# One 128-wide f32 product in place of two 64-wide ones, in a two-layer decoder trunk

## Chip, cores and metric

The kernel runs on one core of a Trainium2 chip. The metric is the device time of one execution in microseconds; lower is better. All arithmetic is in f32.

## What is computed

A trunk of two layers over 1024 tokens of width 1024. Layer 0 mixes by causal pooling, layer 1 by sliding-window attention; both attend to 256 memory tokens as well, and both end in a squared-ReLU MLP of width 4096. Cut to the products:

```
for l in range(2):
    if l == 1:
        kv = rmsnorm(h, kv_norm) @ w_kv                     # 1024x1024 @ 1024x512
    proj = rmsnorm(h, norm_mix[l]) @ w_in[l]                # 1024x1024 @ 1024x1024
    main, mq = proj[..., :768], proj[..., 768:]
    main_out = pool_mixer(main, ...) if l == 0 else swa_sink_attention(rmsnorm(main), k, v, sinks)
    mkv = rmsnorm(mem, mem_norm[l]) @ w_mem_kv[l]           # 256x1024 @ 1024x512
    mem_out = memory_attention(rmsnorm(mq), mk, mv)
    h = h + concat([main_out, mem_out]) @ w_out[l]          # 1024x1024 @ 1024x1024
    u = relu(rmsnorm(h, norm_mlp[l]) @ w_up[l])             # 1024x1024 @ 1024x4096
    h = h + (u * u) @ w_down[l]                             # 1024x4096 @ 4096x1024
```

## The kernel before

Activations lie transposed: 128 features on the partitions, tokens along the free dimension, in halves of 512 tokens. A product takes a weight tile of 128 inputs (partitions) by 128 outputs as the stationary operand and 512 tokens as the moving one, and adds into one bank of 128 outputs by 512 tokens. All such products go through one helper, `pair` (lines 259 to 261). It issues two matmuls, one for outputs 0 to 63, one for outputs 64 to 127, with the two halves of the weight tile and the same moving operand. Two such matmuls are called a couple here, and one matmul 64-wide by its output partitions.

Four places call it. `mm3` (line 263) runs over the input tiles k of a projection. `scores` (line 501) makes the attention scores of two heads, with 512 or 256 columns. `Stream.run` (line 893) does the MLPs and the output projection of layer 0, in seven products of blocks for eight (the order of the seven steps is `ORDER`, line 611), each unit being four couples. `plain_unit` (line 1009) does the first block of each MLP. The columns number 512, but 256 in the memory projections (`mem_layer`, 413) and in some score products.

Not all of TensorE's work goes through `pair`. Transposes are 128 wide (`transpose4`, line 273; lines 357, 445, 454, 1111). `head_stats` (line 531), `Norm.finish` (line 309) and line 435 reduce over partitions by plain f32 products 128 wide with one or two columns. The products of attention weights and values (line 587 for memory, line 1464 for the window) are written out as 64-wide matmuls, one for each head of a couple of heads.

In `Stream.run` the order of all instructions is written by hand (`tc.manual_schedule`). In the mixing stages they are placed by the framework's scheduler from the order of the code; there the short tasks of attention (`mem_attn`, `swa`, `head_stats`) are interleaved with projections by `tick`, which every couple calls with 0.43.

Of the kernel before, what the change touches and what calls it, by code (L numbers as in the profile page):

```python
# [16 lines left out]
P = 128  # L17
# [23 lines left out]
def kernel(  # L41
# [25 lines left out]
    nc = tc.nc  # L67
# [56 lines left out]
    def mm_tile():  # L124
        return mmps.tile([P, HALF], F32, tag="mm", name="mm")
# [27 lines left out]
    for wi in range(4):  # L153
        w = 2 << wi
# [102 lines left out]
    ALL = slice(0, P)  # L257

    def pair(ps, w, a, start, stop, **kw):
        for e in (slice(0, 64), slice(64, P)):  # L260
            nc.tensor.matmul(ps[e], w[:, e], a, start=start, stop=stop, **kw)  # L261

    def mm3(ps, wsel, asel, ks, us=0.43):

        n = len(ks)
        for i, k in enumerate(ks):
            w0, a0 = wsel(k, 0), asel(k, 0)
            pair(ps, w0, a0, i == 0, i == n - 1)
            tick(us)
# [231 lines left out]
    def scores(ps, st, n, khi):  # L501

        t = slice((n % 2) * P, (n % 2 + 1) * P)
        pair(ps, st[:, 0, t], khi, True, True)
# [155 lines left out]
    class Stream:  # L660
# [232 lines left out]
        def run(self, plain=()):  # L893
# [5 lines left out]
            for i in range(-len(plain), n):  # L899
# [22 lines left out]
                for k in range(4):  # L922
                    x_ = step.win[k]
                    pair(ps, w[:, 0, k, :], x_[:, 0], m in (1, 2, 7) and k == 0, k == 3, skip_group_check=True)
                    tick(0.43)
# [589 lines left out]
    for n in range(NK):  # L1515
# [6 lines left out]
        for hf in range(2):  # L1522
            ps = mm_tile()
# [10 lines left out]
    for n in range(NK):  # L1534
# [4 lines left out]
        for hf in range(2):  # L1539
            ps = mm_tile()  # L1540
# [41 lines left out]
```

## Time and profile before

| | us |
|---|---|
| median of the runs (2, from 2356.3 to 2357.81) | 2357.06 |
| the profiled execution | 2354.09 |
| its span, first to last instruction | 2352.3 |
| TensorE busy in it | 2326.8 |
| ScalarE busy | 989.6 |
| VectorE busy | 797.9 |
| GpSimd busy | 168.8 |

The span is what the profile covers. A matmul counts as busy from its start to a modelled end, and matmuls overlap, so starts tell more than busy time. PE is TensorE's matmuls, PEld its weight loads, DVE is VectorE, ACT is ScalarE, SP issues most DMAs. A row's shape "128*64 128x512" is: stationary operand of 128 partitions by 64 columns, moving operand of 128 partitions by 512 columns.

### The profile page before, as it was taken

What the parts mean: (1) busy time and instruction counts of PE and PEld (TensorE: products, weight loads), DVE (VectorE), ACT (ScalarE), POOL (GpSimd) and SP (SyncE); (2) the same over time, 40 slices, a digit from 0 to 9 for tenths busy, and PEclk for the clock granted to TensorE, in tenths of its full rate; (3) what the DMA queues carried; (4) which work ended last, traced back from release to release, by engine and by line L of the source; (5) the groups of instructions that cost most, each with busy time, mean ns of one, the idle gap of its engine ahead of it and who ended that gap; (6) DMA issues with size and microseconds to landing.
All of it is one profiled execution on the core that took longest, in us unless ns stands there. A gap on an engine that the chain in (4) does not pass through costs nothing.

```text
span 2352.3 us, 28640 instructions
## 1 busy us (share of the span) xinstructions
PE 2326.8 (99%) x11324; PEld 847.8 (36%) x11324; DVE 797.9 (34%) x1495; ACT 989.6 (42%) x2063; POOL 168.8 (7%) x226
## 2 busy tenths in 40 slices
PE   8999899999999999999999999999999999999999
PEld 4543233333333333333444443333333333333333
DVE  1363425322232152153243443433521422233141
ACT  6443454533532442454343464545423523532442
POOL 1410020000000000000322120020000000000000
PEclk9999999999999999999999999999999999999999
DMA  5302312223213213211211031214132133113201
GB/s 215 90 23 87 108 54 108 89 90 105 74 54 113 85 36 126 90 59 43 70 39 35 27 97 51 86 55 147 42 125 90 37 106 108 55 62 118 90 18 54
DMA packets 139064, 185.99 MB, mean 79 GB/s; under 512 B 20852, under 2 KB 67762, under 8 KB 138930
## 3 DMA queue, kind: packets, MB, share of 16 engines
q1 hardware_dynamic: 137458, 179.43, 23.3%
q10 hardware_dynamic: 1472, 4.73, 0.5%
q8 instruction: 90, 1.47, 0.3%
q14 instruction: 44, 0.36, 0.1%
HBM read 152.67 MB, written 31.46 MB: 78 GB/s over the span
## 4 chain that ended last, share of the span: by engine, by line
PE 97%; ACT 1%; DVE 1%; DMA 1%; issue 0%; SPq 0%; ACTq 0%
PE mm L261 54%; PE sps L261 26%; PE pv L261 12%; PE tr L273 2%; PE tr L531 1%; PE pv L1464 1%; PE pv L587 1%; PE tr L309 0%; DMA wa<-in_w_out 0%; ACT s L1431 0%; DMA g<-in_x 0%; ACT s L568 0%; ACT qs L230 0%; ACT x L230 0%; DVE g L1195 0%
## 5 line engine op out<-in xcount | busy, mean ns | idle before, releaser
L261 PE MATMUL mm<-x,w 128*64 128x512 f32 x4640 | 1071.8, 595 | 3.3 <-DVE h L370 2.1
L261 PEld LDWEIGHTS mm<-x,w 128*64 128x64 f32 x4640 | 338.1, 137 | 627.9 <-issue 607.6
L261 PE MATMUL sps<-x,w 128*64 128x512 f32 x1920 | 429.5, 592 | 0.0
L637 ACT ACTIVATE w<-wa 128x512 f32<-128x512 f32 x371 | 230.5, 623 | 452.0 <-PE mm L261 198.2
L261 PEld LDWEIGHTS sps<-x,w 128*64 128x64 f32 x1920 | 137.6, 137 | 272.5 <-issue 268.8
L261 PE MATMUL pv<-x,w 128*64 128x512 f32 x976 | 220.2, 592 | 0.0
L949 DVE TENSOR_TENSOR wa<-wa 128x512 f32<-128x512 f32 x264 | 176.5, 687 | 29.8 <-ACT w L637 22.4
L957 DVE TENSOR_TENSOR h<-mm,h 128x512 f32<-128x512 f32 x124 | 85.7, 691 | 282.7 <-PE mm L261 282.7
L261 PE MATMUL mm<-x,g 128*64 128x512 f32 x736 | 167.3, 592 | 0.0
L999 DVE TENSOR_TENSOR g<-mm,g 128x512 f32<-128x512 f32 x48 | 33.2, 692 | 341.1 <-PE mm L261 341.1
L980 ACT ACTIVATE g<-g 128x512 f32<-128x512 f32 x90 | 56.7, 630 | 152.7 <-DVE g L999 152.7
L957 DVE TENSOR_TENSOR h<-sps,h 128x512 f32<-128x512 f32 x84 | 58.1, 691 | 182.6 <-PE sps L261 182.6
L261 PEld LDWEIGHTS pv<-x,w 128*64 128x64 f32 x976 | 69.9, 137 | 138.5 <-issue 136.5
L637 ACT ACTIVATE x<-g 128x512 f32<-128x512 f32 x192 | 114.3, 614 | 0.9 <-PE mm L261 0.9
L261 PE MATMUL sps<-x,g 128*64 128x512 f32 x480 | 109.0, 592 | 0.0
L261 PE MATMUL mm<-g,w 128*64 128x512 f32 (+1 forms) x564 | 100.9, 504 | 7.0 <-ACT w L637 7.0
L250 POOL TENSOR_TENSOR raw<-raw,cols 128x512 f32<-128x512 f32 x40 | 43.3, 1100 | 787.0 <-DMA raw<-in_w_in 739.4
L261 PEld LDWEIGHTS mm<-x,g 128*64 128x64 f32 x736 | 52.9, 137 | 105.1 <-issue 103.9
L230 ACT ACTIVATE w<-raw 128x512 f32<-128x512 f32 (+1 forms) x80 | 46.5, 583 | 70.7 <-PE mm L261 43.3
L984 ACT ACTIVATE g<-g 128x512 f32<-128x512 f32 x120 | 73.9, 616 | 0.0
L999 DVE TENSOR_TENSOR g<-sps,g 128x512 f32<-128x512 f32 x30 | 20.8, 692 | 150.5 <-PE sps L261 150.5
L994 ACT ACTIVATE g<-mm 128x512 f32<-128x512 f32 x42 | 25.1, 597 | 102.8 <-PE mm L261 102.8
(226 smaller groups left out, 1797.8 us busy)
## 6 DMA issues: line engine op xcount, KB each, us to landing
x<-win SPq DMA_DIRECT2D x168, 256.0 KB, 2.9
wa<-in_w_up SPq DMA_DIRECT2D x32, 1024.0 KB, 6.2
wa<-in_w_down SPq DMA_DIRECT2D x32, 1024.0 KB, 5.1
win<-x SPq DMA_DIRECT2D x56, 256.0 KB, 2.0
h<-hd SPq DMA_DIRECT2D x16, 512.0 KB, 5.5
raw<-in_w_in SPq DMA_DIRECT2D x10, 512.0 KB, 3.7
g<-in_x SPq DMA_DIRECT2D x8, 512.0 KB, 6.5
raw<-in_w_mem_kv SPq DMA_DIRECT2D x8, 512.0 KB, 3.9
```

Source lines behind the costliest of these rows:

```text
L230: nc.scalar.activation(dst[:, 0], src, AF.Copy)
L250: nc.gpsimd.tensor_tensor(r, r, gain[:, k0:k0 + n].rearrange("p (k o) -> p k o", o=1).broadcast_to([P, n, P]), op=ALU.mult)
L261: nc.tensor.matmul(ps[e], w[:, e], a, start=start, stop=stop, **kw)
L273: nc.tensor.transpose(dst_ps[:, i * P:(i + 1) * P], s, ident)
L531: nc.tensor.matmul(st[:, 2 * j:2 * j + 2], sq[:, j * P:(j + 1) * P], blk2, start=True, stop=True)
L637: nc.scalar.activation(dst[:, 0], src, AF.Copy)
L949: eng.tensor_tensor(out_, a, b, op=op)
L957: nc.vector.tensor_tensor(c, ps, c, op=ALU.add)
L980: nc.scalar.activation(c, c if src is None else src, AF.Relu)
L984: nc.scalar.activation(c, c, AF.Square)
L994: nc.scalar.activation(c, ps, AF.Copy)
L999: nc.vector.tensor_tensor(c, ps, c, op=ALU.add)
```

## The change

The loop over the two halves in `pair` goes; one matmul takes the whole weight tile and writes the whole bank. The line numbers behind it fall by one (L261 becomes L260, L273 becomes L272, L587 becomes L586).

```
     def pair(ps, w, a, start, stop, **kw):
-        for e in (slice(0, 64), slice(64, P)):
-            nc.tensor.matmul(ps[e], w[:, e], a, start=start, stop=stop, **kw)
+        nc.tensor.matmul(ps, w, a, start=start, stop=stop, **kw)
```

In the mixing stages the scheduler also moves instructions. On PE, in the first projection of the kernel (memory queries, `mm`), among the transposes of the second half of x (`g` into `tr`, `mm`, `sps`), there stands before:

```order
L261 MATMUL mm<-x,w 64x512 x2
L1111 MATMUL tr<-ident,t 128x52
L1130 MATMUL tr<-sink_row,ones_row 128x12
L261 MATMUL mm<-x,w 64x512
L273 MATMUL tr<-ident,g 128x128 x8
L261 MATMUL mm<-x,w 64x512
L273 MATMUL mm<-ident,g 128x128 x4
L273 MATMUL tr<-ident,g 128x128 x4
L261 MATMUL mm<-x,w 64x512
L273 MATMUL tr<-ident,g 128x128 x4
L261 MATMUL mm<-x,w 64x512 x3
```

and in the changed kernel:

```order
L260 MATMUL mm<-x,w 128x512
L1110 MATMUL tr<-ident,t 128x52
L1129 MATMUL tr<-sink_row,ones_row 128x12
L260 MATMUL mm<-x,w 128x512
L272 MATMUL tr<-ident,g 128x128 x8
L272 MATMUL mm<-ident,g 128x128 x4
L272 MATMUL tr<-ident,g 128x128 x4
L260 MATMUL mm<-x,w 128x512
L272 MATMUL tr<-ident,g 128x128 x4
L260 MATMUL mm<-x,w 128x512
```

The halves of two couples stood apart, with transposes between them; now a product stands whole, and twelve transposes follow the first eight without a product between.

On PE, in the memory attention of layer 0 (`s` are attention weights being transposed, `pv` the products with the values, `mkh` the keys, `x` and `w` a projection running alongside), there stands before:

```order
L273 MATMUL tr<-ident,s 128x128 x8
L261 MATMUL mm<-x,w 64x512 x4
L273 MATMUL tr<-ident,s 128x128 x4
L261 MATMUL mm<-x,w 64x512
L273 MATMUL tr<-ident,s 128x128 x4
L261 MATMUL mm<-x,w 64x512
L587 MATMUL pv<-pt,mkv 64x128 x8
L261 MATMUL mm<-x,w 64x512 x4
L587 MATMUL pv<-pt,mkv 64x128 x8
L261 MATMUL sps<-mkh,qs 64x512 x4
```

and in the changed kernel:

```order
L272 MATMUL tr<-ident,s 128x128 x8
L260 MATMUL mm<-x,w 128x512 x2
L272 MATMUL tr<-ident,s 128x128 x4
L260 MATMUL mm<-x,w 128x512
L272 MATMUL tr<-ident,s 128x128 x4
L586 MATMUL pv<-pt,mkv 64x128 x8
L260 MATMUL mm<-x,w 128x512 x2
L586 MATMUL pv<-pt,mkv 64x128 x8
L260 MATMUL sps<-mkh,qs 128x512 x2
```

The couple that was split by four transposes stands whole before them, and the value products, still 64 wide, now stand between 128-wide work on both sides.

## Rows read from the trace of the kernel before

**Rows 1.** The page, parts 1 and 2: TensorE's busy time and granted clock

```profile
PE 2326.8 (99%) x11324; PEld 847.8 (36%) x11324; DVE 797.9 (34%) x1495; ACT 989.6 (42%) x2063; POOL 168.8 (7%) x226
...
PEclk9999999999999999999999999999999999999999
```

**Rows 2.** The page, part 4: the chain that ended last, by engine

```profile
PE 97%; ACT 1%; DVE 1%; DMA 1%; issue 0%; SPq 0%; ACTq 0%
```

**Rows 3.** Waits of PE, first and last of ten: us, times, longest

```profile
PE mm L261 <- ACT w L637: 7.0, 1, 7.0
...
PE tr L273 <- ACT t L1551: 0.3, 1, 0.3
```

**Rows 4.** Groups by shape on PE: count | busy us, mean ns | idle before

```profile
L261 PE MATMUL mm<-g,w 128*64 128x256 f32 x256 | 30.9, 384 | 0.0
...
L531 PE MATMUL tr<-blk,t 128*128 128x2 f32 x192 | 24.4, 249 | 0.0
...
L445 PE MATMUL tr<-ident,t 128*128 128x128 f32 x8 | 1.8, 300 | 0.0
```

**Rows 5.** Groups by shape of the weight loads: 64 wide, transposes, 128 wide

```profile
L261 PEld LDWEIGHTS mm<-x,w 128*64 128x64 f32 x4640 | 338.1, 137 | 627.9 <-issue 607.6 <-ACT x L230 4.8 <-ACT w L637 2.6
...
L273 PEld LDWEIGHTS tr<-ident,s 128*128 128x128 f32 x224 | 24.5, 143 | 31.2 <-issue 10.6 <-ACT pt L545 7.0 <-DVE s L1441 3.2
L531 PEld LDWEIGHTS tr<-blk,t 128*128 128x128 f32 x192 | 23.3, 191 | 10.6 <-issue 6.4 <-ACT pt L545 1.3 <-ACT s L1431 0.8
```

**Rows 6.** Time line of weight loads, 1000 to 1004 us: start, length, group, count

```profile
1000.23 0.14 PEld L261 LDWEIGHTS mm<-x,w 128*64 128x64 f32 x2 [0.29 <-issue]
...
1003.66 0.14 PEld L261 LDWEIGHTS mm<-x,g 128*64 128x64 f32 x2 [0.28 <-issue]
```

**Rows 7.** Time line of PE, 29 to 42 us: start, length, group, count of records

```profile
29.32 1.94 PE L261 MATMUL mm<-x,w 128*64 128x512 f32 x8
31.19 0.66 PE L273 MATMUL sps<-ident,g 128*128 128x128 f32 x4
31.77 1.08 PE L261 MATMUL mm<-x,w 128*64 128x512 f32 x4
32.78 0.26 PE L1111 MATMUL tr<-ident,t 52*128 52x52 f32 x1
...
33.29 1.07 PE L261 MATMUL mm<-x,w 128*64 128x512 f32 x2
34.29 1.09 PE L273 MATMUL tr<-ident,g 128*128 128x128 f32 x8
35.31 1.07 PE L261 MATMUL mm<-x,w 128*64 128x512 f32 x2
```

**Rows 8.** Time line of PE, 91 to 94 us

```profile
91.27 0.44 PE L445 MATMUL tr<-ident,t 128*128 128x128 f32 x2
91.64 1.07 PE L261 MATMUL mm<-x,w 128*64 128x512 f32 x2
92.64 0.44 PE L454 MATMUL tr<-ident,ys 128*128 128x128 f32 x2
92.91 0.95 PE L531 MATMUL tr<-blk,t 128*128 128x2 f32 x8
93.80 6.65 PE L261 MATMUL mm<-x,w 128*64 128x512 f32 x29
```

**Rows 9.** Time line of PE, 118 us: a broken couple beside value products

```profile
118.06 0.64 PE L261 MATMUL mm<-x,w 128*64 128x512 f32 x1
118.07 0.65 PE L587 MATMUL pv<-pt,mkv 128*64 128x128 f32 x4
118.55 0.59 PE L261 MATMUL mm<-x,w 128*64 128x512 f32 x1
```

**Rows 10.** Busy us (records) by engine, 330 to 1160 us; granted clock; DMA

```profile
330.00:1160.00 830.00, 830.00 (x3906) 283.76 (x3904) 260.78 (x375) 331.94 (x597) 27.30 (x27) 1.00 0.24 81
```

**Rows 11.** The same for line 261 alone (PE, PEld), whole span

```profile
0.00:2352.30 2352.30, 2202.87 (x10152) 732.33 (x10152) 1.00 0.24 79
```

## The prediction

> **What bounds the kernel now.** I read the page first. TensorE is busy for 99% of the span at a granted clock of 9 or more tenths in every slice, which is the 2.4 GHz level [rows 1], and the chain that ended last is 97% TensorE [rows 2]. The list of waits says how little idles: ten rows, from 7.0 us down to 0.3 us, 21.4 us in all [rows 3]. So only what TensorE's own instructions take can move the end.
>
> Next, the groups by shape, to see what one product is on the chip. The memory projections issue 64 couples, that is 128 products, of 256 columns (2 layers, 4 units, 8 steps): their group holds 256 records. The 96 products of L531 (24 calls of `head_stats`, 4 each), which are plain f32 products 128 wide, have 192 records, while the 8 transposes of L445 have 8 [rows 4]. So a plain f32 product is two records, each with its own weight load, whether 64 or 128 wide; a transpose is one.
>
> Then the time line of the weight loads in a dense stretch: two loads (one for each half of the couple) start together, and the next two 0.43 us later; from 1000.23 to 1003.66 are eight such steps, 0.429 us each [rows 6]. A couple is two such rounds, 0.86 us. The time line of the matmuls confirms it and shows the decisive thing [rows 7]. Eight records (two couples) hold TensorE from 29.32 to 31.19, 1.87 us; four (one couple) from 31.77 to 32.78, 1.01 us; so one couple more costs 0.86 us, and a stretch of couples costs 0.15 us on top. At 33.29 stands one 64-wide product alone, its partner put off behind transposes: two records, until 34.29, 1.00 us. **One 64-wide product alone takes as long as the couple.** The halves of a couple run side by side on two halves of the array, and what is paid for is two streamings of the 512 columns, however many of the 128 output partitions are filled.
>
> **The change, part by part.**
>
> *The products.* All 10,152 records of L261 [rows 11] are 5,076 products, 2,538 couples: by PE's order 2,456 with 512 columns and 82 with 256. Now: 2,456 x 2 x 0.429 + 82 x 2 x 0.215 = 2,142 us. Afterwards 2,538 products, again two records each, 5,076 rounds. A round has no reason to take longer: the columns streamed are the same. No row shows a 128-wide plain product with 512 columns, so I bound it. The transposes are 128 wide: four of them, with the return, take 0.58 us (31.19 to 31.77), eight 1.02 us (34.29 to 35.31), so 0.11 us each, with a load of 0.143 us within [rows 5, 7]; full-width loading is hidden there even behind a short stream. The plain 128-wide load takes 0.191 us against 0.137 us for 64 [rows 5], under half of a 0.43 us stream. I take 0.429 us and a change of nothing; the load's cover is the stream of the round before it. A step of 2 ns in the round, up or down, would be 10 us. If the cover is gone, it costs 0.11 us in each of 5,076 rounds (first rival).
>
> *The changes of width.* Where 64-wide work meets 128-wide work, time is lost on both sides. On the 64-wide side it is the 0.15 us above. On the other side, four transposes in 0.58 us instead of 4 x 0.11 lose 0.14 us. That this belongs to the width, not to the kind of work, shows at 91 us [rows 8]: two transposes followed by couples last 0.37 us (91.27 to 91.64), two followed by the 128-wide products of L531 only 0.27 us (92.64 to 92.91). Behind L531 the way back is cheap: eight records take 0.89 us with it (92.91 to 93.80), 0.11 each. By PE's order, TensorE changes width 226 times before and 72 times after; what is left are 36 stretches of the value products (L1464 and L587), still 64 wide. At 0.15 us each, 154 changes are 23 us; I take off 5 us for the cheap ones at L531 and L309 (some 35, half price), and put back 2 us, since on leaving each of the 36 the longer load stands uncovered (0.191 - 0.137 = 0.054 us each). Gain 20 us. Ends: 0, if the loss is not one of width, and 25.
>
> *The broken couples.* In 24 stretches of 64-wide work an odd number of products stands, because transposes or value products split a couple; a product alone costs a round pair for half the work (33.29 to 34.29), so 24 x 0.43 = 10 us. Afterwards no couple can be split. In places the empty half was used by value products, where a lone record and four of L587 run at once (118.06 to 118.55) [rows 9], so less may come back: ends 6 and 20 us, the latter if the halves lost time against each other throughout those mixed stretches. I take 10.
>
> *The rest.* The order on the SP queue is unchanged, so every transfer is issued behind the same ones. VectorE and ScalarE change places of a few instructions in the mixing stages; their cost I set at nothing, because TensorE hides them: in the long MLP stretch from 330 to 1160 us VectorE is busy 261 and ScalarE 332 of 830 us [rows 10]. There, where TensorE has no idle time at all and hardly changes width, I expect nothing but the price of the round: 830 us again within 3. In the attention stages some of the saved time will turn into waits for softmax; that costs at most what is gained there.
>
> **Sum.** 20 + 10 = 30 us off the profiled execution's 2,354.1 us (its span of 2,352.3 and 1.8 around it) gives 2,324. The median of the runs is 2,357.1, 3 us more; against it the forecast is **2,327 us**, 1.3% less. A measurement tells about 2% from no change, so this counts as the same.
>
> **Rivals.**
>
> 1. *The 128-wide load is not covered (slower).* If the next load has to wait until the stream has left the array, each of 5,076 rounds grows by the 0.11 us at which L531's products follow each other, which is the pace of the bare load: + 558 us, less the 30: 2,885 us. From 16 ns a round the change is slower by over 2% (16 x 5,076 = 81 us, against 30 + 47). For it: the only plain 128-wide products here have one or two columns, and show no load beneath a stream. Against it: transposes, which load at full width beneath a stream of 128 columns. The Trainium skill (TensorE: Matmul & The Clock Gate, Part 3, "The mechanism") says that loads overlap running matmuls only with another row group; every load here uses all rows, so by that sentence none would be hidden, and this would be the result. The trace disagrees for the 64-wide loads and the transposes, hence a chance of only 7%.
>
> 2. *Halves side by side are really faster (much slower).* If a 128-wide product streamed its columns twice as often as a 64-wide one, each couple's 0.86 us would double: 2,357 + 2,142, some 4,500 us. The lone product speaks against it: it fills half of the array in the time of the couple, and L531 has two records for its 128-wide products as well. The Trainium skill (TensorEngine Tiling (Array Packing), "Theoretical Speedup") promises up to 2x for tiles of 64 columns; the trace agrees (two products in the time of one), but that is a gain over a half-empty array, not over a full one. 3%.
>
> 3. *No gain.* The 0.15 us stays, being the price of going from products to transposes, or comes back as waits for softmax: 2,350 to 2,358 us. 13%.
>
> 4. *More gain.* The whole 25 and 20 us, and a round shorter by 1 ns: 2,357 - 50 = 2,307 us, faster by over 2%. 8%.
>
> **How the numbers follow.** The forecast, 2,312 to 2,345 us, has 69%. With the third and most of the fourth rival the range is 2,300 to 2,360. Faster by over 2% (below 2,310): 0.08. Slower (above 2,404): 0.10. The same: 0.82.
>
> **What would show it.** Line 260 with 5,076 records, each starting 0.43 us after the one before, and loads of 0.19 us inside; transposes behind a product 0.43 us after its last record's start, not 0.52; the MLP stretch as long as now. Rounds of 0.45 us or more, or idle time of the load queue gone, would prove the first rival; MLP stretches of twice the length the second; rows of waits for ScalarE or VectorE adding up to some 50 us instead of 21 the third.

## Result and profile after

The changed kernel takes 2,324.6 us (2 runs, 2,324.4 and 2,324.7) against 2,357.1; the ratio is 0.986, 95% interval 0.982 to 0.9905. It is faster by 1.4%, 32.5 us, which is less than the 2% that the prediction called the same. The forecast was 2,327 us. The profiled executions differ by 29.6 us in span, since that of before was 3 us below its median; what follows explains these 29.6.

The head of the page of the changed kernel (parts 1, 2 and 4, to be laid beside [rows 1, 2]):

```profile
span 2322.7 us, 18466 instructions
...
PE 2292.3 (99%) x6248; PEld 1070.7 (46%) x6248; DVE 797.9 (34%) x1495; ACT 988.9 (43%) x2063; POOL 167.9 (7%) x226
...
PEclk9999999999999999999999999999999999999999
...
PE 95%; DVE 1%; DMA 1%; ACT 1%; POOL 1%; issue 0%; SPq 0%; ACTq 0%; POOLq 0%
```

TensorE still binds at 99%, with 6,248 records instead of 11,324; the span is 29.6 us shorter. The busy time of the weight loads has grown by 223 us, and no wait in the list further down names them.

Busy time of the product line alone over the whole span (PE, then PEld, with the number of records; to [rows 11]):

```profile
0.00:2322.70 2322.70, 2176.28 (x5076) 953.99 (x5076) 1.00 0.24 80
```

Groups of weight loads by shape in the changed kernel (to [rows 5]), and its time line of loads in a dense stretch (to [rows 6]):

```profile
L260 PEld LDWEIGHTS mm<-x,w 128*128 128x128 f32 x2320 | 433.7, 190 | 518.8 <-issue 508.6 <-ACT x L230 2.4 <-DVE h L369 2.4
```

```profile
999.99 0.19 PEld L260 LDWEIGHTS sps<-x,w 128*128 128x128 f32 x1 [0.24 <-issue]
...
1003.86 0.19 PEld L260 LDWEIGHTS mm<-x,w 128*128 128x128 f32 x1 [0.24 <-issue]
```

From 999.99 to 1003.86 are nine steps, 0.430 us each by these rounded times. Over a longer stretch there is no difference to the 0.429 of before: from the 750th to the 2,250th round of 512 columns both kernels take 643.75 us, by the starts of all records. In each round the load takes 0.19 us instead of 0.14, and then the load queue stands idle for 0.24: the load is covered by the stream.

The time line of TensorE in the first projection (to [rows 7]):

```profile
38.70 0.60 PE L272 MATMUL sps<-ident,g 128*128 128x128 f32 x4
39.13 1.88 PE L260 MATMUL mm<-x,w 128*128 128x512 f32 x4
40.85 0.60 PE L272 MATMUL mm<-ident,g 128*128 128x128 f32 x4
41.29 1.02 PE L260 MATMUL mm<-x,w 128*128 128x512 f32 x2
```

Four transposes now take 0.43 us (38.70 to 39.13) where they took 0.58, and two products 1.72 (39.13 to 40.85) where two couples took 1.87. Both losses of 0.15 us are gone.

The same pattern can be read undisturbed at the end of the program, where transposes of the output stand between groups of eight rounds. Before:

```profile
2315.35 0.66 PE L273 MATMUL tr<-ident,h 128*128 128x128 f32 x4
2315.94 1.08 PE L261 MATMUL mm<-x,w 128*64 128x512 f32 x4
2316.85 2.75 PE L261 MATMUL sps<-x,w 128*64 128x512 f32 x12
2319.52 0.66 PE L273 MATMUL tr<-ident,h 128*128 128x128 f32 x4
```

After:

```profile
2288.16 0.60 PE L272 MATMUL tr<-ident,h 128*128 128x128 f32 x4
2288.60 1.02 PE L260 MATMUL mm<-x,w 128*128 128x512 f32 x2
2289.46 2.74 PE L260 MATMUL sps<-x,w 128*128 128x512 f32 x6
2292.03 0.60 PE L272 MATMUL tr<-ident,h 128*128 128x128 f32 x4
```

One period was 4.17 us and is 3.87: eight rounds and four transposes, both times, and 0.30 us for going there and back between the widths, which is gone.

A place where changes of width are left, at the value products of the memory attention:

```profile
109.73 0.60 PE L272 MATMUL tr<-ident,s 128*128 128x128 f32 x4
110.26 1.09 PE L586 MATMUL pv<-pt,mkv 128*64 128x128 f32 x16
111.28 1.98 PE L260 MATMUL mm<-x,w 128*128 128x512 f32 x4
113.20 1.09 PE L586 MATMUL pv<-pt,mkv 128*64 128x128 f32 x16
```

Sixteen records of 64-wide value products take 1.02 us (110.26 to 111.28), 0.15 more than their eight rounds of 0.109; the four wide records behind them take 1.92 us instead of 1.72 (111.28 to 113.20), 0.20 more. So a stretch of value products costs 0.35 us of changes.

The waits of TensorE, the longest five of thirteen (to [rows 3]):

```profile
PE mm L260 <- ACT w L636: 7.6, 1, 7.6
PE mm L356 <- POOL mkh L477: 4.7, 1, 4.7
PE tr L272 <- DVE s L1440: 4.3, 3, 2.5
PE mm L260 <- DVE h L369: 2.1, 1, 2.1
PE tr L272 <- DVE cols L1111: 1.6, 1, 1.6
```

All thirteen add up to 26.1 us; the ten of before to 21.1 (the prediction's 21.4 was a slip in adding). Five microseconds of the gain came back as waits.

Where the time went, by first and last record of three lines in both kernels:

```profile
L587 PE MATMUL pv<-pt,mkv x256: 272/273/324, 118.1 to 1257.7; 128*64 128x128 f32 x128
...
L1464 PE MATMUL pv<-pt,g x88: 486/486/900, 1324.0 to 1518.9; 128*64 128x384 f32 x88
...
L309 PE MATMUL tr<-ones,t x48: 250/250/271, 338.6 to 1570.6; 128*128 128x1 f32 x48
```

```profile
L586 PE MATMUL pv<-pt,mkv x256: 272/273/324, 110.3 to 1239.2; 128*64 128x128 f32 x128
...
L1463 PE MATMUL pv<-pt,g x88: 486/486/538, 1303.6 to 1494.3; 128*64 128x384 f32 x88
...
L308 PE MATMUL tr<-ones,t x48: 167/250/250, 329.5 to 1545.6; 128*128 128x1 f32 x48
```

At the first value products the changed kernel leads by 7.8 us, at the first norm behind layer 0's mixing by 9.1, at the last value products of layer 1 by 24.6, and at the end by 29.6. The rest of layer 0, its MLP included, adds 1 us: at the norm behind that MLP the lead is 10.2 us (time line of both kernels):

```profile
1126.93 0.38 PE L309 MATMUL tr<-ones,t 128*128 128x1 f32 x2
```

```profile
1116.72 0.28 PE L308 MATMUL tr<-ones,t 128*128 128x1 f32 x2
```

Some 14 us more come in the mixing of layer 1. The second MLP adds 5 us, and the tail of its output transposes alone explains most of that (13 groups, 0.30 us each).

### The profile page after: what moved, and what is told of

It is laid out like the page before. It is cut to its first block, busy times and chain, and to the rows that moved or that the text cites. A ratio compares the mean times of both kernels' runs of the same rounds, so it can differ in the third digit from the quotient of the medians.

```text
span 2322.7 us, 18466 instructions
## 1 busy us (share of the span) xinstructions
PE 2292.3 (99%) x6248; PEld 1070.7 (46%) x6248; DVE 797.9 (34%) x1495; ACT 988.9 (43%) x2063; POOL 167.9 (7%) x226
## 4 chain that ended last, share of the span: by engine, by line
PE 95%; DVE 1%; DMA 1%; ACT 1%; POOL 1%; issue 0%; SPq 0%; ACTq 0%; POOLq 0%
PE mm L260 53%; PE sps L260 26%; PE pv L260 12%; PE tr L272 2%; PE pv L1463 1%; PE tr L530 1%; PE pv L586 1%; DMA g<-in_x 1%; PE tr L308 0%; DMA wa<-in_w_out 0%; POOL hpw L538 0%; POOL raw L250 0%; DMA raw<-in_w_in 0%; ACT s L567 0%; DVE t L1208 0%
## 5 line engine op out<-in xcount | busy, mean ns | idle before, releaser
L260 PE MATMUL mm<-x,w 128*128 128x512 f32 x2320 | 1041.0, 594 | 2.9 <-DVE h L369 2.1
L260 PEld LDWEIGHTS mm<-x,w 128*128 128x128 f32 x2320 | 433.7, 190 | 518.8 <-issue 508.6
L260 PE MATMUL sps<-x,w 128*128 128x512 f32 x960 | 428.6, 592 | 0.0
L260 PEld LDWEIGHTS sps<-x,w 128*128 128x128 f32 x960 | 182.1, 190 | 227.7 <-issue 226.7
L260 PE MATMUL pv<-x,w 128*128 128x512 f32 x488 | 219.7, 592 | 0.0
L260 PE MATMUL mm<-x,g 128*128 128x512 f32 x368 | 166.9, 592 | 0.0
L260 PEld LDWEIGHTS pv<-x,w 128*128 128x128 f32 x488 | 92.6, 190 | 115.8 <-issue 115.0
L260 PEld LDWEIGHTS mm<-x,g 128*128 128x128 f32 x368 | 69.9, 190 | 88.0 <-issue 87.8
L260 PE MATMUL mm<-g,w 128*128 128x512 f32 (+1 forms) x282 | 101.4, 509 | 7.6 <-ACT w L636 7.6
L260 PE MATMUL sps<-x,g 128*128 128x512 f32 x240 | 108.7, 592 | 0.0
L260 PEld LDWEIGHTS mm<-g,w 128*128 128x128 f32 x282 | 53.5, 194 | 48.6 <-issue 37.5
```

What stands on the lines that cost most here:

```text
L260: nc.tensor.matmul(ps, w, a, start=start, stop=stop, **kw)
```

## Experiments

My theory: a round takes 0.429 us at either width, and the gain comes from changes of width and from broken couples. Its rivals: the wide round itself is shorter; each half pays for itself; the wide load is not covered; the loss belongs to transposes and not to the width.

**One part alone: the streams.** `whole` is the new `pair` under another name.

```
 in Stream.run and plain_unit:
-    pair(ps, w..., x_...)
+    whole(ps, w..., x_...)
```

> 128-wide products in the hand-ordered MLP streams alone, couples in the projections and the scores. Theory (a round takes 0.429 us at either width; what is gained is changes of width and broken couples): PE's order has 186 changes of width instead of 226, so 40 x 0.10 to 0.15 = 4 to 6 us less, 2,352 us, and records of the product line still 0.429 us apart. Rival (the wide round itself is a little shorter, and that is where the 32 us come from): three quarters of all rounds are here, so some 24 us less, 2,333 us.

Measured: 2,348.1 us against 2,356.1, ratio 0.9969 (0.9958 to 0.998), 8 us less. The theory said 4 to 6, the rival 24. The rival falls: three quarters of the rounds became wide and gave a quarter of the gain, and 1,500 of these wide rounds take the same 643.75 us as before. The interval, 5 to 10 us, takes in the upper end of the theory.

**The other part alone: projections and scores.**

```
 in mm3 and scores:
-    pair(ps, ...)
+    whole(ps, ...)
```

> The other part alone: 128-wide products in the projections and the scores, couples in the MLP streams. Theory: 118 changes of width instead of 226 and 6 odd stretches instead of 24; 108 x 0.13 + 18 x 0.43 = 22 us less, and some more where couples ran out of step beside value products: 2,331 us (2,326 to 2,336). Rival (the wide round is shorter): 8 us less, 2,349 us.

Measured: 2,331.8 us, ratio 0.9897 (0.9882 to 0.9912), 24 us less, as the theory said. The two parts together, 8 + 24, are the whole change.

**Couples unbroken.** The second half of a couple gets a priority 60 places earlier with the scheduler, in projections and scores.

```
 in mm3 and scores, through a helper:
+    nc.tensor.matmul(ps[0:64], w[:, 0:64], a, ...)
+    with tc.high_priority(offset=60):
+        nc.tensor.matmul(ps[64:P], w[:, 64:P], a, ...)
```

> Couples everywhere; in the projections and the scores the second half is only given a better place with the scheduler, so that a couple is seldom split: 6 odd stretches instead of 24, still 226 changes of width. Theory: a product alone costs the 0.86 us of a couple, so 18 x 0.43 = 8 us less, 2,349 us (2,346 to 2,353). Rival (the split couples cost nothing, since other work fills the empty half, and all of the gain is in the changes of width): 2,357 us.

Measured: 2,341.9 us, ratio 0.994 (0.9926 to 0.9955), 14 us less, nearly twice what I expected and outside my range. The rival falls, but my size was off. Where the time went I read from all records of the time line: the length of each stretch of 64-wide work, less its rounds (two halves side by side count as one), 0.15 us of changes and the listed waits. In the 88 stretches of couples alone this was 7.4 us before and nothing here (-0.5); 15 of the 24 odd stretches stood there, and none does now. In the stretches where couples and value products are mixed (24 before, 23 here) it was 16.4 us before and 10.2 here, with only four odd ones fewer. My reading is that a product alone leaves the two halves of the array out of step, and that one half is paid for empty until the end of the stretch; counting odd stretches misses this where the value products make the count even again. The 6 us are measured, but no run isolates this cause of them.

**Changes of width with nothing else.**

```
 in Stream.run, unit i:
-    pair(ps, ...)
+    (whole if i % 2 else pair)(ps, ...)
```

> In the hand-ordered streams every second unit takes 128-wide products, the others couples: 672 changes of width instead of 226, all of them between products of the same 512 columns, with no transposes near. Theory (0.15 us lost per change of width, and 0.05 us more on each entry to the wide side for its longer load): 446 x 0.15 + 223 x 0.05 = 78 us more, 2,435 us (2,420 to 2,445). Rival (the loss belongs to going from products to transposes, not to the width): 2,350 to 2,357 us.

Measured: 2,431.2 us, ratio 1.0318 (1.0301 to 1.0335), 75 us more; the theory said 78. Time line of TensorE in this run, where line 264 is the wide product and line 261 the couple:

```profile
602.01 3.70 PE L264 MATMUL mm<-x,w 128*128 128x512 f32 x8
605.64 3.65 PE L261 MATMUL mm<-x,g 128*64 128x512 f32 x16
609.22 3.27 PE L264 MATMUL mm<-x,w 128*128 128x512 f32 x7
```

Both stretches are eight rounds, 3.43 us. The wide one takes 3.63 (602.01 to 605.64), 0.20 more, the one of couples 3.58 (to 609.22), 0.15 more. There are no transposes here: the loss belongs to the width. The weight loads at these two entries:

```profile
602.00 0.30 PEld L264 LDWEIGHTS mm<-x,w 128*128 128x128 f32 x2 [0.81 <-issue]
...
605.64 0.20 PEld L261 LDWEIGHTS mm<-x,g 128*64 128x64 f32 x4 [0.76 <-issue]
```

At either entry the load queue has been idle for 0.8 us instead of some 0.25, and the first load starts together with its product: no stream covers it. The 0.05 between the two prices is the difference of the two loads (0.191 and 0.137 us).

**Half of a couple left out.**

```
 in Stream.run:
+    (lower if m == 5 else pair)(ps, ...)    # lower: the first of pair's two matmuls
```

> Couples as before, but in one of the seven block products of the streams (m = 5, 264 couples) only the lower half is issued; the upper 64 outputs of that block product are left out. Theory (a product alone takes the two streamings of the couple): no time is saved, 2,357 us as before (2,353 to 2,360), TensorE's records there 0.43 us apart. Rival 2 (each half pays for itself): 264 x 0.43 = 113 us less, 2,243 us.

Measured: 2,354.1 us, the kernel before on the same chip 2,358.1. Half of the work of 264 couples is gone, and of the time 4 us, which is as much as runs of the kernel before differ among themselves (2,353.5 to 2,357.2 in ten). Time line, line 264 being the product alone:

```profile
586.64 3.60 PE L264 MATMUL mm<-x,w 128*64 128x512 f32 x8
590.07 3.60 PE L264 MATMUL mm<-x,g 128*64 128x512 f32 x8
593.51 3.60 PE L264 MATMUL mm<-x,w 128*64 128x512 f32 x8
```

Eight records of four products alone take 3.43 us, what eight pairs of records of four couples take.

**Both halves on the same side.**

```
 in Stream.run, for m == 5:
-    nc.tensor.matmul(ps[e], w[:, e], a, ...)
+    nc.tensor.matmul(ps[0:64], w[:, e], a, ...)
```

> Couples as before, but for m = 5 both products of a couple go to the lower half of the array and of the bank, so that the outputs of that block product are wrongly summed there and the upper ones left out. Theory (halves run side by side only because they are different halves; on the same half they follow each other): 264 x 0.86 = 227 us more, 2,584 us. Rival (the chip would overlap any two such products, or the halves never overlapped and the couple was paid one after the other): 2,357 us.

Measured: 2,580.4 us, 222 more; the theory said 227. Four couples in this form:

```profile
421.19 7.03 PE L265 MATMUL sps<-x,w 128*64 128x512 f32 x16
428.06 7.03 PE L265 MATMUL pv<-x,w 128*64 128x512 f32 x16
```

6.87 us instead of 3.43. So these 64-wide products run side by side only on different halves, and the couples before the change did so. Here the halves of the array and of the bank change together; the run does not tell which of the two decides.

**The cover of the wide load taken away.** Eight pieces of 64 columns, on the changed kernel.

```
 in Stream.run, for m == 5:
-    pair(ps, w, a, start, stop)
+    for c in range(0, HALF, 64):
+        pair(ps[:, c:c + 64], w, a[:, c:c + 64], start, stop)
```

> 128-wide products as in the changed kernel, but for m = 5 each is issued in eight pieces of 64 columns, each loading its weights again. Theory (a stream of 2 x 64 columns, 0.056 us, no longer covers the 128-wide load, whose bare pace is 0.112 us): 264 products x 16 rounds x 0.112 = 473 us in place of 226, so 247 us more than the changed kernel, 2,571 us. This is the price of rival 1 where the cover is really gone. Rival (the wide load runs ahead in any case): 264 x 16 x 0.056 = 237, 2,335 us.

Measured: 2,569.3 us, 245 more than the changed kernel; the theory said 247.

```profile
411.30 7.25 PE L260 MATMUL sps<-x,w 128*128 128x64 f32 x64
418.39 7.31 PE L260 MATMUL pv<-x,w 128*128 128x64 f32 x64
```

64 records in 7.09 us (411.30 to 418.39), 0.111 us each: the pace of the load, as in L531, twice the 0.054 us that 64 columns would take at the pace of the long ones (an eighth of 0.429). The number of instructions is not what binds: the next run issues twice as many and is faster. Load and stream still overlap: one after the other they would take 0.11 + 0.05 us. So a round takes the longer of the two, and this run is not yet the first rival, in which the load would be added to the stream, though the expectation calls it so.

**The same pieces in couples,** on the kernel before.

> The same eight pieces of 64 columns for m = 5, but in couples as before the change. Theory (each half loads only 64 columns, 0.054 us, both at once, so load and stream are about equal): 264 x 16 x 0.058 = 245 us in place of 226, some 20 us more than the kernel before, 2,376 us (to 2,400), so that here couples would be some 200 us better than whole products. Rival (the number of instructions binds at this length, or loads of the two halves queue behind each other, 0.112 us a round): 2,604 us.

Measured: 2,387.4 us, 29 more than the kernel before; the theory said 20.

```profile
411.45 3.90 PE L261 MATMUL sps<-x,w 128*64 128x64 f32 x128
415.18 4.15 PE L261 MATMUL pv<-x,w 128*64 128x64 f32 x127
```

128 records are 64 rounds, 3.73 us (411.45 to 415.18), 0.058 us each. Here the couple is nearly twice as fast as the whole product, because each half loads 64 columns and the two loads run at the same time. With this one block product in pieces, the kernel of couples is 182 us faster than the kernel of whole products.

**What is left in the waits.** Two versions of the changed kernel count a projection's product as more time in the interleaving.

```
-    def mm3(ps, wsel, asel, ks, us=0.43):
+    def mm3(ps, wsel, asel, ks, us=0.86):    # second version: 0.6
```

> The changed kernel, with the step that a product of a projection counts for in the interleaving of attention tasks set to what it takes (0.86 and 0.43 instead of 0.43 and 0.22): the tasks come back after half as many products. It tells whether waits left over from the mixing stages (26 us by the profile of the changed kernel, of which some 13 in attention) can be moved by it. Theory: TensorE's rounds and nearly all changes of width stay (76 instead of 72), so only the waits can change, within 2,315 to 2,335 us; most likely more waits, since softmax has fewer products to hide behind: 2,328 us. Rival: attention ends sooner and the waits at the ends of its stages go: 2,318 us.

> The same with 0.6 and 0.3, half way. Theory: 2,326 us, between the changed kernel and the run with 0.86; rival: 2,320 us.

Measured: 2,327.7 us, ratio to the kernel before 0.9877 (0.986 to 0.9895), and 2,323.1 us, 0.9858 (0.984 to 0.9876). Neither differs from the changed kernel's 0.986 by more than its interval, so they decide nothing between theory and rival. The largest wait is the same in the profile of 0.86:

```profile
PE mm L260 <- ACT w L636: 7.9, 1, 7.9
```

No version here beats the changed kernel measurably.

## Why the prediction was right

A budget of the span puts the steps side by side. Work is the sum of all rounds at the measured paces (0.429, 0.216, 0.323 and 0.109 us for 512, 256, 384 and 128 columns, 0.109 for a transpose, 0.112 for the narrow products); it is the same in all three. Changes of width are counted stretches at 0.30 us there and back, somewhat less at L531 and L309, and 0.35 for those left after the change. What remains is broken couples and the rest, which holds TensorE's time at a lower clock as well.

| us | before | couples unbroken | changed |
|---|---|---|---|
| span | 2,352.3 | 2,340.2 | 2,322.7 |
| work | 2,265.3 | 2,265.3 | 2,265.3 |
| before the first and after the last record's start | 9.0 | 9.1 | 9.1 |
| changes of width | 31 | 31 | 12 |
| listed waits, without the first | 16.6 | 19.8 | 21.4 |
| remainder | 30 | 15 | 15 |

The prediction read the granted clock by the page's slices of nearly 60 us [rows 1], in which short stretches at the lower level do not show. After the longest wait (7.6 us, until 235.62) the changed kernel's rounds take 0.854 us each until 241; the granted clock there is 0.50, the level of 1.2 GHz. Two loads, five rounds apart, and the stretch from 235 to 241 us (granted clock third from the end):

```profile
236.63 0.34 PEld L260 LDWEIGHTS mm<-g,w 128*128 128x128 f32 x1 [0.52 <-issue]
...
240.90 0.34 PEld L260 LDWEIGHTS mm<-g,w 128*128 128x128 f32 x1 [0.52 <-issue]
```

```profile
235.00:241.00 6.00, 5.38 (x7) 2.29 (x8) 0.00 (x0) 2.75 (x5) 0.00 (x0) 0.50 1.04 392
```

The kernel before has the same behind its wait of 7.0 us (granted clock 0.50 from 245.9 to 249.1). In the first projection, behind a wait of 1.6 us for `cols`, the changed kernel has it again (0.50 from 33.0 to 36.4), where sixteen transposes stand in a row: eight behind the first eight, not twelve as said with the order above. Over all stretches in which the granted clock is 0.50, rounds take 4.8, 3.0 and 4.5 us more in the three kernels than at the full clock. It hardly touches the comparison of before and changed, but of the 15 us by which keeping couples together lowered the remainder nearly 2 belong to it. The rest of the remainder is not split up here.

- **The products cost the same.** Shown: 1,500 rounds take 643.75 us before and after, in the MLP of layer 0; the streams alone gave 8 us instead of 24. That a lone product takes the time of a couple, read from one place at 33 us [rows 7], held for 264 couples.
- **Changes of width, 20 us.** The budget gives 19, and alternating widths confirmed both prices, 0.15 us a change and 0.05 us for the uncovered load.
- **Broken couples, 10 us (6 to 20).** Too small: 15 by the budget, 14 by the run that only kept couples together, of which nearly 2 are clock. The step that failed in size is the count of odd stretches: the mixed stretches, which stood in the prediction only as the upper end, gave about 6 us beside it. That their halves were out of step is argued, not shown.
- **Waits.** The prediction let saved time in the attention stages turn into waits and put no number on it. They took back 5 us (16.6 to 21.4), which is why 19 + 15 did not become more than 30. Neither version with a larger step in `tick` got them back measurably.
- **Rivals.** The uncovered load (7%) did not come: the load of 0.19 us runs beneath a stream of 0.43 us. Even at 64 columns the round was the load's 0.111 us, not load and stream added. The second rival fell with the half that was left out. "No gain" fell with the alternating widths. "More gain" did not come: 19 and 15 us instead of 25 and 20, waits against them, and no shorter round.

So the mechanism was right, but that the total was hit so closely is luck: 5 us too little in one term and 5 us of waits not counted in another cancelled each other.

The Trainium skill (TensorEngine Tiling (Array Packing), "Key Properties") says that changing the tiling mode drains the TensorE, without a price. The traces agree with that: at a change the next load is not ahead of its product, and the change costs 0.15 us, 0.20 us into 128-wide f32 products. The sentence of the Trainium skill that loads overlap only matmuls of another row group (TensorE: Matmul & The Clock Gate, Part 3, "The mechanism"), taken alone, does not describe these traces: the products' loads use all 128 rows, and they run beneath the stream. The same section names a background weight buffer as another way; whether that is what hides the loads, no run here shows.

## What to carry to other kernels

Before packing two narrow products side by side, find one that runs alone in the trace: if it takes as long as the couple, a single wide product costs the same, has no halves that can be torn apart, and needs no change of array width next to transposes and other wide work. The narrow form pays where the stream is shorter than the weight load (here, in f32, at 64 columns: 0.058 against 0.111 us a round; lengths between 64 and 512 were not compared). Price such a change by counting width changes and broken couples in the order, and expect part of the gain back as waits in stages that were just covered.

## What was not expected of the hardware

After products that stood alone, the halves stay out of step. In the run with the lower half alone, the couples behind such products start their halves apart; its time line of TensorE:

```profile
606.44 0.59 PE L261 MATMUL mm<-x,g 128*64 128x512 f32 x1
606.81 0.59 PE L261 MATMUL mm<-x,w 128*64 128x512 f32 x1
606.87 3.54 PE L261 MATMUL mm<-x,g 128*64 128x512 f32 x14
609.87 0.59 PE L261 MATMUL sps<-x,w 128*64 128x512 f32 x1
```

One half begins a unit (`g`, 606.44) before the other has begun the last record of the unit before (`w`, 606.81), and still eight rounds take 3.43 us (606.44 to 609.87). Where the time of the empty half is lost, no run separates.

And work of the other half may start between the two records of a lone product: four records of value products start from 118.07 on, between the records at 118.06 and 118.55 [rows 9].
